# The last four weight chunks of a routed expert block: half of their pieces issued from ScalarE's DMA queue

## Chip, cores and metric

One NeuronCore of a Trainium2 chip runs the whole program. The metric is device time in microseconds (us); a version is timed in several runs, and the median counts. TensorE (PE) multiplies, VectorE (DVE) and ScalarE (ACT) do elementwise work, GpSimd (POOL) little, SyncE (SP) only issues DMA transfers. The profile's times count from the start of the span.

## What is computed

One encoder layer over 512 tokens of width 1024: token mixers, a layer norm, then a mixture of 32 SwiGLU experts, two for each token, and a second layer norm. The change touches the experts alone:

```python
def expert_block(args):
    tok, wgt, e = args
    xb = t[tok]
    hb = jax.nn.silu(xb @ w_gate[e]) * (xb @ w_up[e])
    return (hb @ w_down[e]) * wgt[:, None].astype(xb.dtype)
...
return _layer_norm(ALPHA * h + ffn, ln2_g[layer], ln2_b[layer])
```

All 32 experts are used, each with 6 MB of float32 weights (gate and up 1024 x 512, down 512 x 1024).

## The kernel before

**Rounds.** The experts are taken in 15 rounds (`PER`, L32): two or four experts a round share the 128 rows of the PE array. The last round, p = 14, has four experts with 32 token slots each. A round is: gather its tokens, gate projection, up projection (`gate_up`, L1175), silu and product (`glu`), transposes, the down projection in two halves of 512 output columns, and adding the results to the tokens' rows (`combine`).

**Chunks.** The weights come in chunks of 1 MB, 192 in all, numbered in the order of use; the last round has chunks 168 to 191: eight of gate (168 to 175), eight of up (176 to 183), four for the first down half (184 to 187) and four for the second (188 to 191). A gate or up chunk holds half of one expert's rows. PE takes the row blocks k = 0 to 3 of all four experts first (chunks 176 to 179 of up), then k = 4 to 7 (180 to 183). `chunk_load` (L713) issues a chunk: gate and up as one transfer of 1 MB (L726), chunks 184 to 187 as two halves of 512 KB (L738), and chunks 188 to 191 as four pieces of 256 KB each (L743): halves `kk` = 0, 1 and in each two pieces `j` = 0, 1, a piece being 256 rows x 256 columns of one expert. `PLACE[p] + 2 * kk + j` is the piece's place in the experts' order; which expert stands there is known only at run time, so `expert` (L703) loads its number from the tile `cnti` into a register of SP (a TENSOR_LOAD, L707).

**Buffers.** Chunks go round a ring of SBUF buffers (`ring_at`); from chunk 174 on, a chunk takes the buffer of the chunk 14 before it. Chunks 188 and 189 take those of gate chunks 174 and 175 (tiles sX and craw), 190 and 191 those of up chunks 176 and 177 (two tiles sS). A load waits until PE has read the older chunk. `load_after(n)` (L781) issues, in the program's order, all loads whose buffer is free once the chunks below n are used; `gate_up` calls it after gate (m = 0) and after up (m = 1), `pair` after the down halves.

**Queue and semaphores.** All these loads are issued by SP, in order. The DMA transfers of the program take eight semaphores (DMAHW0 to DMAHW7) in turn, and each transfer's issue waits until the transfer that had its semaphore before has landed; so eight are in flight at most, and an issue that waits holds back all issues behind it on its engine.

**The end.** `last_round` (L1502) prepares the rows of the second layer norm (four small casts on ACT, `row_parts`), then slot numbers, silu and product, three spread rows that ACT copies (L1520), transposes, the first down half (`down_mm`, chunks 184 to 187), its combination, and the second half in four column blocks (`columns`, L1540, chunks 188 to 191), one chunk each. `finish` does the layer norm and stores.

Of the kernel before, what the change touches and what calls it, by code (L numbers as in the profile page):

```python
# [24 lines left out]
E = 32  # L25
# [10 lines left out]
PLACE = [sum(PER[:p]) for p in range(len(PER))]  # L36
# [7 lines left out]
def dram(ap, offset, dims):  # L44
    return bass.AP(tensor=ap.tensor, offset=ap.offset + offset, ap=dims)
# [3 lines left out]
def hybrid_block(ctx: ExitStack, tc: tile.TileContext, x, w_in, b_in, sg_ln_g, sg_ln_b, sg_w, sg_b,  # L49
# [3 lines left out]
    nc = tc.nc  # L53
# [618 lines left out]
    def ring_at(i):  # L672
        if i < 22:
            return ring[i - 2]
        if i >= LAST:
            return ring_at(LAST - 14 + (i - LAST) % 14)
        return (ring[:13] + ["raw"] + ring[13:])[(i - 22) % AHEAD]
# [14 lines left out]
    NP = len(PER)  # L692
    order = [(p, c) for p in range(NP) for c in range(6 * PER[p])]
    where = {pc: i for i, pc in enumerate(order)}

    def wide(i):
        p, c = order[i]
        return p > 0 and (c < 4 * PER[p] or p < NP - 1)

    ids = {}  # L700


    def expert(place):  # L703
        if place < FIXED:
            return slice(place, place + 1)
        if place not in ids:
            ids[place] = nc.values_load(  # L707
                cnti[0:1, E + 1 + place:E + 2 + place], engines=[mybir.EngineType.SP], min_val=0, max_val=E - 1,
                skip_runtime_bounds_check_because="a sum of a one-hot column's products with 0 to 31")
        return ds(ids[place], 1)  # L710


    def chunk_load(dst, i, kk):  # L713
        p, c = order[i]
        n = PER[p]
        if wide(i):
            e, part = expert(PLACE[p] + c % n), c // n % 2
            src = w_down if c >= 4 * n else (w_gate, w_up)[c // (2 * n)]
            dst = dst.rearrange("p k a b -> p (k a b)" if kk is None else "p a b -> p (a b)")
            run = dst.shape[1]  # L720
            at = run * kk if kk else 0
            if c >= 4 * n:
                rows, at = slice(0, FF), at + 2048 * part
            else:
                rows = slice(512 * part, 512 * part + 512)
            nc.sync.dma_start(dst, src[0][e, rows, :].rearrange("o (p i) f -> p (o i f)", i=4)[:, at:at + run])  # L726
            return
        if p == 0 and c < 8:
            nc.sync.dma_start(dst, dram((w_gate, w_up)[c // 4], (2 * p * D + 256 * (c % 4) + 128 * kk) * FF,
                                        [[FF, 128], [D * FF, 2], [1, FF]]))  # L730
        elif p == 0:
            nc.sync.dma_start(dst, dram(w_down, (2 * p * FF + 256 * (c % 2) + 128 * kk) * D + 512 * ((c - 8) // 2),
                                        [[D, 128], [FF * D, 2], [1, 512]]))
        else:
            m, q = (c - 16) // 4, c % 4
            if m == 0:
                w, r = w_down[0][expert(PLACE[p] + 2 * (q % 2) + kk)], 256 * (q // 2)
                nc.sync.dma_start(dst, w[:, r:r + 256, 0:512].rearrange("o (k p) f -> p (o k) f", p=128))  # L738
            else:
                r, f = 256 * (q % 2), 512 + 256 * (q // 2)  # L740
                for j in range(2):
                    w = w_down[0][expert(PLACE[p] + 2 * kk + j)]
                    nc.sync.dma_start(dst[:, j].rearrange("p (k f) -> p k f", f=256),  # L743
                                      w[:, r:r + 256, f:f + 256].rearrange("o (k p) f -> p (o k) f", p=128))

    held, whole = {}, {}
# [34 lines left out]
    def load_after(n):  # L781
        if 24 <= n < len(order):
            i = max(chunks) + 1
            while i < len(order) and max(v for v in chunks if v > 1 and ring_at(v) == ring_at(i)) < n:
                load_chunks(i, i + 1)
                i += 1
# [72 lines left out]
    cnti = const.tile([1, 2 * E + 1], I32, name="cnti")  # L859
# [315 lines left out]
    def gate_up(p, xe, filler=None):  # L1175
        pg, pu = bank("acc"), bank("acc")
        n = PER[p]
        w = 128 // n
        for m, o in enumerate((pg, pu)):

            ks = range(8) if p or m else (3, 4, 5, 0, 1, 6, 2, 7)
            for k in ks:
                if filler and m and k % 2:
                    filler(k // 2)
                for j in range(n):
                    P.matmul(o[j * w:(j + 1) * w, :], lhsT=xe[:, k, j * w:(j + 1) * w],  # L1186
                             rhs=chunk(p, m, j, k), start=k == ks[0], stop=k == ks[-1],
                             skip_group_check=True)
            if p == 1:
                load_chunks(32 + 5 * m, 37 + 4 * m)  # L1190
            load_after(where[p, 2 * n * (m + 1) - 1] + 1)
        return pg, pu

    with tc.manual_schedule():
# [76 lines left out]
    def glu(pg, pu, scale=1.0 / WSCALE):  # L1271
        sl = mw.tile([128, FF], F32, name="sl", tag="olo")
        S.activation(sl, pg, AF.Silu)  # L1273
        V.scalar_tensor_tensor(sl, sl, scale, pu, op0=OP.mult, op1=OP.mult)  # L1274
        return sl
# [226 lines left out]
    def last_round(gu, ohf):  # L1502
        G.memset(ones_r.bitcast(F32), 1.0)
        G.memset(zero_b, 0.0)
        p = NP - 1
        l2 = ln2_params()

        spare = [spare_at(i) for i in range(1, 3)]
        for tag in spare:
            held.pop(tag, None)  # L1510
        v, more = [slot(tag, F32R) for tag in spare]
        ov = [(v[:, 0], v[:, 1]), (v[:, 2], v[:, 3])]
        parts = [row_parts(l2[j // 2][0:1, j % 2], *[w[0:1] for w in places])
                 for j, places in enumerate(ov + [(more[:, 0], more[:, 1]), (more[:, 2], more[:, 3])])]
        tid, ws = slot_info(p, ohf, "acc")
        sl = glu(*gu)
        for j in range(3):
            pb = bank("acc")
            spread(parts[j], pb)
            S.copy(l2[j // 2][:, j % 2], pb)  # L1520
        hT = glu_transpose(sl, "acc", wide=False)
        ohT = token_hot(tid)
        S.activation(warm2, eps_c, AF.Sqrt)

        def split_out(n, po, cs):
            oh, ol = [w[:, cs] for w in ov[n]]
            S.activation(oh, po[:, cs], AF.Copy, scale=ws)
            V.scalar_tensor_tensor(ol, po[:, cs], ws, oh.bitcast(F32), op0=OP.mult, op1=OP.subtract)

        def combine1(cs, stop=False):  # L1530
            for h in range(2):
                for t in range(NT):
                    P.matmul(pc[t][:, cs], lhsT=ohT[:, t * 128:(t + 1) * 128], rhs=ov[1][h][:, cs],
                             start=False, stop=stop and h == 1, skip_group_check=True)

        def columns(po, m):
            cs = slice(256 * (m // 2), 256 * (m // 2) + 256)
            for k in range(m % 2 * 2, m % 2 * 2 + 2):
                for j in range(4):
                    P.matmul(po[j * 32:(j + 1) * 32, cs], lhsT=hT[:, k, j * 32:(j + 1) * 32],  # L1540
                             rhs=chunks[where[p, 20 + m]][j // 2][:, j % 2, k % 2 * 256:k % 2 * 256 + 256],
                             start=k == 0, stop=k == 3, skip_group_check=True)

        most, rest = slice(0, 256), slice(256, 512)
        split_out(0, down_mm(p, 0, hT), slice(0, 512))
        for t in range(NT):
            p0 = bank("acc")
            for h in range(2):
                P.matmul(p0, lhsT=ohT[:, t * 128:(t + 1) * 128], rhs=ov[0][h], start=h == 0, stop=h == 1)
            V.tensor_add(y[t][:, 0:512], y[t][:, 0:512], p0)  # L1550
            V.bn_stats(st2[t][:, 0], y[t][:, 0:512])
        po = [bank("acc"), bank("acc")]
        pz = [bank("acc") for _ in range(2)]
        columns(po[0], 0)
        for t in range(2):
            spread(parts[3], pz[t], skip_group_check=True)
        columns(po[0], 1)
        split_out(1, po[0], most)
        columns(po[1], 2)
        combine1(most)  # L1560
        for t in range(NT):
            V.bn_stats(st2[t][:, 1], pc[t][:, most])
        pz += [bank("acc") for _ in range(2)]
        spread(parts[3], pz[2], skip_group_check=True)
        columns(po[1], 3)
        split_out(1, po[1], rest)
        combine1(rest, stop=True)
        spread(parts[3], pz[3], skip_group_check=True)
        return l2, pz
# [107 lines left out]
```

## Time and profile before

| | us |
|---|---|
| median of 3 runs (934.21 to 934.65) | 934.59 |
| the profiled execution | 934.43 |
| its span | 932.9 |
| PE busy in the span | 891.9 (96%) |
| DVE, ACT, POOL busy | 430.9, 292.8, 58.0 |
| mean DMA rate over the span | 275 GB/s |

The span holds the program's instructions; the 1.5 us between it and the execution's time lie around it. Busy shares are means over stages with different limits, so a change at the very end is read from the rows of the last 75 us. In the chain of waits, a row is a stretch of work or of waiting that the end hangs on; a DMA in it counts from its issue to its landing. Matmul rows show the engine's start of a group and, in brackets, how long it sat idle before and what ended that.

### The profile page before, as it was taken

How to read it: one execution, taken by the hardware profiler on the slowest of the kernel's cores; microseconds unless marked ns; L12 is line 12 of the kernel's file. 1: busy time of each engine (PE TensorE's matmuls, PEld its weight loads, DVE VectorE, ACT ScalarE, POOL GpSimd, SP SyncE). 2: the span in 40 equal slices, each digit the busy share in tenths (PEclk: the TensorE clock that was granted, in tenths of full speed). 3: DMA queues.
4: the chain of work that ended last, by engine and by line, in shares of the span. 5: the costliest groups of instructions: out<-in, count | busy, mean ns of one | idle time of the engine just before them, and what ended most of it. 6: DMA issues, size and time to landing. Idle time of an engine off the chain costs nothing. (4 is left out here: it accounts for less than half of the span.)

```text
span 932.9 us, 13620 instructions
## 1 busy us (share of the span) xinstructions
PE 891.9 (96%) x5215; PEld 577.4 (62%) x5216; DVE 430.9 (46%) x912; ACT 292.8 (31%) x526; POOL 58.0 (6%) x114
## 2 busy tenths in 40 slices
PE   8999999999999999999999999799999999978786
PEld 6989898986888888888834544344444444422132
DVE  4567675767963243244778422322333223401216
ACT  4456575667841242133361101110111011100112
POOL 6010101001010020020000000000000000000002
PEclk9999999999999999999999999899999999988899
DMA  8635343533233386874688999999999999999993
GB/s 227 169 100 145 97 136 96 136 113 102 69 98 95 89 319 217 290 259 160 260 293 340 402 417 410 416 419 419 418 420 419 420 420 418 418 418 420 420 359 142
DMA packets 79446, 256.11 MB, mean 275 GB/s; under 512 B 8984, under 2 KB 30544, under 8 KB 58384
## 3 DMA queue, kind: packets, MB, share of 16 engines
q1 hardware_dynamic: 78064, 252.36, 71.7%
q0 software_dynamic: 1312, 2.83, 1.5%
q8 instruction: 43, 0.70, 0.3%
q14 instruction: 27, 0.22, 0.1%
HBM read 244.67 MB, written 2.10 MB: 265 GB/s over the span
## 5 line engine op out<-in xcount | busy, mean ns | idle before, releaser
L119 DVE TENSOR_TENSOR sW<-wraw,sW 128x1024 fp32r<-128x1024 f32 (+1 forms) x38 | 46.5, 1224 | 98.4 <-ACT sW L118 98.3
L118 ACT CAST sW<-wraw 128x1024 fp32r<-128x1024 f32 (+1 forms) x38 | 39.1, 1030 | 116.9 <-PE ps_w L144 63.3
L1186 PE MATMUL ps_acc<-sS,xe 128*64 128x512 f32 (+1 forms) x192 | 65.9, 613 | 8.0 <-PEq L1317 5.8
L142 PE MATMUL ps_acc<-sX,sW 128*128 128x512 f32 x184 | 73.3, 398 | 0.0
L144 PE MATMUL ps_acc<-sX,sW 128*128 128x512 f32 x184 | 72.3, 393 | 0.0
L143 PE MATMUL ps_acc<-sX,sW 128*128 128x512 f32 x184 | 72.0, 391 | 0.0
L1260 DVE TENSOR_REDUCE tid<-ps_w 128x1 f32<-128x2 f32 x12 | 1.9, 158 | 139.4 <-PE ps_w L1255 139.4
L1303 DVE SCALAR_TENSOR_TENSOR olo<-ps_acc,ws,ohi 128x512 fp32r<-128x512 f32 x24 | 18.0, 750 | 99.3 <-ACT ohi L1302 99.3
L1313 DVE TENSOR_TENSOR h<-h,ps_w 128x512 f32<-128x512 f32 x96 | 59.4, 679 | 8.5 <-PE ps_w L1310 8.5
L1186 PE MATMUL ps_acc<-sW,xe 128*64 128x512 f32 (+1 forms) x152 | 60.6, 617 | 1.4 <-DMA sW<-in_w_up_dram 1.4
L1186 PE MATMUL ps_acc<-sO,xe 128*64 128x512 f32 (+1 forms) x224 | 59.6, 594 | 0.0
L1302 ACT ACTIVATE ohi<-ps_acc,ws 128x512 fp32r<-128x512 f32 x24 | 16.5, 687 | 130.5 <-PE ps_acc L1293 117.9
L1245 PEld LDWEIGHTS <-hs 128*128 128x128 f16 x768 | 44.5, 98 | 19.8 <-issue 19.6
L1186 PE MATMUL ps_acc<-sX,xe 128*64 128x512 f32 (+1 forms) x152 | 47.9, 645 | 4.3 <-DMA sX<-in_w_up_dram 3.4
L1245 PE MATMUL ps_acc<-oh,hs 128*128 128x128 f16 x768 | 51.1, 220 | 0.0
L1186 PE MATMUL ps_acc<-sE,xe 128*64 128x512 f32 (+1 forms) x176 | 48.9, 594 | 1.3 <-DMA sE<-in_w_up_dram 1.3
L262 DVE TENSOR_TENSOR sW<-wraw,sW 128x1024 fp32r<-128x1024 f32 x31 | 38.3, 1241 | 11.0 <-ACT sW L258 10.3
L1186 PEld LDWEIGHTS ps_acc<-sS,xe 128*64 128x64 f32 (+1 forms) x192 | 18.1, 129 | 38.2 <-issue 32.2
L1284 ACT COPY hT<-ps_w 128x512 f32<-128x512 f32 x12 | 7.0, 585 | 107.8 <-PE ps_w L1281 107.8
L1273 ACT ACTIVATE sl<-ps_acc 128x512 f32<-128x512 f32 x13 | 7.7, 595 | 104.0 <-PE ps_acc L1186 104.0
L1293 PE MATMUL ps_acc<-sS,hT 128*64 128x512 f32 (+1 forms) x96 | 37.3, 627 | 2.2 <-DMA sS<-in_w_down_dram 2.2
L144 PEld LDWEIGHTS ps_acc<-sX,sW 128*128 128x128 f32 x184 | 34.5, 188 | 7.5
(405 smaller groups left out, 2011.2 us busy)
## 6 DMA issues: line engine op xcount, KB each, us to landing
wraw<-in_w_in_dram SPq DMA_DIRECT2D x32, 512.0 KB, 3.7
sO<-in_w_up_dram SPq DMA_DIRECT2D x14, 1024.0 KB, 19.8
sS<-in_w_gate_dram SPq DMA_DIRECT2D x13, 1024.0 KB, 17.3
sX<-in_w_down_dram SPq DMA_DIRECT2D x13, 1024.0 KB, 14.6
sS<-in_w_down_dram SPq DMA_DIRECT2D x12, 1024.0 KB, 17.4
sE<-in_w_gate_dram SPq DMA_DIRECT2D x12, 1024.0 KB, 19.8
sS<-in_w_up_dram SPq DMA_DIRECT2D x11, 1024.0 KB, 17.3
sO<-in_w_gate_dram SPq DMA_DIRECT2D x11, 1024.0 KB, 19.8
```

Of the source, the lines that this page charges most:

```text
L118: S.copy(hi, src)
L119: V.tensor_sub(lo, src, hi.bitcast(F32))
L142: P.matmul(o, lhsT=lh, rhs=rh, start=first, stop=False)
L143: P.matmul(o, lhsT=lh, rhs=rl, start=False, stop=False)
L144: P.matmul(o, lhsT=ll, rhs=rh, start=False, stop=last)
L262: V.tensor_sub(usplit[i][1], uraw[i], usplit[i][0].bitcast(F32))
L1186: P.matmul(o[j * w:(j + 1) * w, :], lhsT=xe[:, k, j * w:(j + 1) * w], rhs=chunk(p, m, j, k), start=k == ks[0], stop=k == ks[-1], skip_grou ...
L1245: P.matmul(pg[d // 4][:, (d % 4) * 128:(d % 4 + 1) * 128], lhsT=part_block(hs[t][j], d), rhs=ohf[:, t], start=d % 4 == 0 and t == 0 and j ...
L1293: P.matmul(po[j * w:(j + 1) * w, :], lhsT=hT[:, k, j * w:(j + 1) * w], rhs=chunk(p, 2 + n, j, k), start=k == 0, stop=k == 3, skip_group_ch ...
L1302: S.activation(oh, po, AF.Copy, scale=ws)
L1303: V.scalar_tensor_tensor(ol, po, ws, oh.bitcast(F32), op0=OP.mult, op1=OP.subtract)
L1313: V.tensor_add(yn, yn, pcs[t])
```

## The change

In chunks 188 to 191 the pieces of the second half (`kk` = 1) are issued by ACT, on ACT's DMA queue; the expert numbers they need are loaded into registers of ACT as well. The first halves stay with SP. In the last round, the loads that become possible after up (chunks 190 and 191) are no longer written behind up in `gate_up`, but in `last_round` behind `glu`, so on ACT they stand after silu.

```diff
-    def expert(place):
+    def expert(place, engine=mybir.EngineType.SP):
         if place < FIXED:
             return slice(place, place + 1)
-        if place not in ids:
-            ids[place] = nc.values_load(
-                cnti[0:1, E + 1 + place:E + 2 + place], engines=[mybir.EngineType.SP], min_val=0, max_val=E - 1,
+        if (place, engine) not in ids:
+            ids[place, engine] = nc.values_load(
+                cnti[0:1, E + 1 + place:E + 2 + place], engines=[engine], min_val=0, max_val=E - 1,
                 skip_runtime_bounds_check_because="a sum of a one-hot column's products with 0 to 31")
-        return ds(ids[place], 1)
+        return ds(ids[place, engine], 1)
...
                 for j in range(2):
-                    w = w_down[0][expert(PLACE[p] + 2 * kk + j)]
-                    nc.sync.dma_start(dst[:, j].rearrange("p (k f) -> p k f", f=256),
+                    queue, engine = ((nc.sync, mybir.EngineType.SP), (nc.scalar, mybir.EngineType.Activation))[kk]
+                    w = w_down[0][expert(PLACE[p] + 2 * kk + j, engine)]
+                    queue.dma_start(dst[:, j].rearrange("p (k f) -> p k f", f=256),
                                       w[:, r:r + 256, f:f + 256].rearrange("o (k p) f -> p (o k) f", p=128))
...
             if p == 1:
                 load_chunks(32 + 5 * m, 37 + 4 * m)
-            load_after(where[p, 2 * n * (m + 1) - 1] + 1)
+            if p < NP - 1 or m == 0:
+                load_after(where[p, 2 * n * (m + 1) - 1] + 1)
...
         sl = glu(*gu)
+        load_after(where[p, 15] + 1)
         for j in range(3):
```

ACT's order in the last round, the change (sO3 and sZ0 take the casts, sl is silu's output; the rows that prepare a transfer's address are left out):

```order
L707 TENSOR_LOAD cnti_2781
...
L744 DMA sX3_3783<-in_w_down_dram 128x2x256 [waits DMAHW4_49,DMAHW0_49,PE_49]
...
L744 DMA sX3_3783<-in_w_down_dram 128x2x256 [waits DMAHW2_49,PE_49]
...
L744 DMA craw_4014<-in_w_down_dram 128x2x256 [waits DMAHW6_49,DMAHW7_49,DMAHW3_49,DMASW7_49]
...
L744 DMA craw_4014<-in_w_down_dram 128x2x256 [waits DMASW0_49,PE_49]
L118 CAST sO3_8027<-sO2_3509 1x512 [waits DMAHW7_49,DMASW1_49]
...
L1275 ACTIVATE sl_8053<-ps_acc_7929 128x512 [waits DVE_49]
...
L744 DMA sS0_4009<-in_w_down_dram 128x2x256 [waits DMAHW7_49,DMAHW1_49,PE_49]
...
L744 DMA sS0_4009<-in_w_down_dram 128x2x256 [waits DMAHW2_49,PE_49]
...
L744 DMA sS1_4011<-in_w_down_dram 128x2x256 [waits DMAHW4_49]
...
L744 DMA sS1_4011<-in_w_down_dram 128x2x256 [waits DMAHW5_49,PE_49]
L1523 COPY sO2_3509<-ps_acc_8064 128x512 [waits PE_49]
```

Before, none of the DMA rows stood there. The semaphores that the eight new transfers take themselves are, in turn, 0, 2, 3, 4 and, behind silu, 1, 2, 4, 5.

SP's order from the second up chunk to the second down chunk, before (sS1 to sE0 are up chunks 177 to 183, sE1 and sE2 down chunks 184 and 185):

```order
L726 DMA sS1_4011<-in_w_up_dram 128x2048 [waits DMAHW0_49,PE_49]
...
L726 DMA sW2_4018<-in_w_up_dram 128x2048 [waits DMAHW1_49,PE_49]
...
L726 DMA sS2_4193<-in_w_up_dram 128x2048 [waits DMAHW2_49,PE_49]
...
L726 DMA sW0_4195<-in_w_up_dram 128x2048 [waits DMAHW3_49,PE_49]
...
L726 DMA sS3_4197<-in_w_up_dram 128x2048 [waits DMAHW4_49,PE_49]
...
L726 DMA sW1_4199<-in_w_up_dram 128x2048 [waits DMAHW5_49,PE_49]
...
L726 DMA sE0_3265<-in_w_up_dram 128x2048 [waits DMAHW6_49,PE_49]
...
L738 DMA sE1_3268<-in_w_down_dram 128x2x512 [waits DMAHW7_49]
...
L738 DMA sE1_3268<-in_w_down_dram 128x2x512 [waits DMAHW0_49,PE_49]
...
L738 DMA sE2_3271<-in_w_down_dram 128x2x512 [waits DMAHW1_49]
```

and the same rows in the change:

```order
L726 DMA sS1_4011<-in_w_up_dram 128x2048 [waits DMAHW1_49,PE_49]
...
L726 DMA sW2_4018<-in_w_up_dram 128x2048 [waits DMAHW5_49,PE_49]
...
L726 DMA sS2_4193<-in_w_up_dram 128x2048 [waits DMAHW6_49,PE_49]
...
L726 DMA sW0_4195<-in_w_up_dram 128x2048 [waits DMAHW7_49,PE_49]
...
L726 DMA sS3_4197<-in_w_up_dram 128x2048 [waits DMAHW0_49,PE_49]
...
L726 DMA sW1_4199<-in_w_up_dram 128x2048 [waits DMAHW3_49,PE_49]
...
L726 DMA sE0_3265<-in_w_up_dram 128x2048 [waits DMAHW6_49,PE_49]
...
L738 DMA sE1_3268<-in_w_down_dram 128x2x512 [waits DMAHW7_49]
...
L738 DMA sE1_3268<-in_w_down_dram 128x2x512 [waits DMAHW0_49,PE_49]
...
L738 DMA sE2_3271<-in_w_down_dram 128x2x512 [waits DMAHW1_49]
```

SP's transfers keep their order, but their semaphores move: ACT's transfers take numbers between them. sW2 now waits for the semaphore of the first half of gate chunk 175, sS3 for that of ACT's first piece, sW1 for ACT's third, and sE2's two halves for ACT's fifth and sixth.

## Rows read from the trace of the kernel before

**Rows 1.** The page's slices: GB/s in 40 equal slices of the span

```profile
GB/s 227 169 100 145 97 136 96 136 113 102 69 98 95 89 319 217 290 259 160 260 293 340 402 417 410 416 419 419 418 420 419 420 420 418 418 418 420 420 359 142
```

**Rows 2.** The chain that ended last, 870 to 933: start us, us, what

```profile
872.75 19.82 DMA sE<-in_w_up_dram
...
892.62 1.05 PE ps_acc L1186 x2
...
897.63 1.00 PE ps_acc L1186 x8
...
901.85 3.69 PE ps_acc L1293 x32
...
915.40 1.04 PE ps_acc L1540 x16
```

**Rows 3.** PE's waits, 895 to 933: line, releaser, us in total, times, longest

```profile
PE ps_acc L1549 <- ACT sO L1527: 0.8, 1, 0.8
...
PE ps_acc L1453 <- DVE h L1550: 0.4, 1, 0.4
```

**Rows 4.** Single DMA issues at 875.12, 892.69, 893.94, 909.42: KB, us to landing

```profile
sE<-in_w_down_dram SPq DMA_DIRECT2D x1, 512.0 KB, 18.8
...
sO<-in_w_down_dram SPq DMA_DIRECT2D x1, 512.0 KB, 10.7
...
sX<-in_w_down_dram SPq DMA_DIRECT2D x1, 256.0 KB, 10.1
...
sS<-in_w_down_dram SPq DMA_DIRECT2D x1, 256.0 KB, 5.4
```

**Rows 5.** Timeline of SP's queue, 872 to 911: start us, us, instruction

```profile
875.12 0.39 SPq L738 DMA_DIRECT2D sE<-in_w_down_dram  x1
...
892.69 0.39 SPq L738 DMA_DIRECT2D sO<-in_w_down_dram  x1
893.94 0.41 SPq L743 DMA_DIRECT2D sX<-in_w_down_dram  x1
...
904.18 5.62 SPq L743 DMA_DIRECT2D sS<-in_w_down_dram  x8
...
909.42 0.37 SPq L743 DMA_DIRECT2D sS<-in_w_down_dram  x1
```

**Rows 6.** Timeline of PE, 845 to 905: start us, us, [idle before and releaser]

```profile
875.24 1.02 PE L1186 MATMUL ps_acc<-sS,xe 128*32 128x512 f32 x2 [0.22 <-DMA sS<-in_w_up_dram]
877.65 1.04 PE L1186 MATMUL ps_acc<-sS,xe 128*32 128x512 f32 x2 [1.38 <-DMA sS<-in_w_up_dram]
880.14 1.92 PE L1186 MATMUL ps_acc<-sW,xe 128*32 128x512 f32 x2 [1.45 <-DMA sW<-in_w_up_dram]
...
892.62 1.05 PE L1186 MATMUL ps_acc<-sE,xe 128*32 128x512 f32 x2 [1.30 <-DMA sE<-in_w_up_dram]
...
903.59 1.90 PE L1293 MATMUL ps_acc<-sO,hT 128*32 128x512 f32 x16
```

**Rows 7.** Line 707, 800 to 933: duration ns min/median/max, first and last start

```profile
L707 SPq TENSOR_LOAD <-cnti x4: 268/270/275, 834.2 to 839.5; - x4
```

**Rows 8.** Timeline of ACT, 840 to 933

```profile
875.06 0.60 ACT L1273 ACTIVATE sl<-ps_acc 128x512 f32<-128x512 f32 x1 [8.95 <-PE ps_acc L1186]
899.61 1.56 ACT L1520 COPY sO<-ps_acc 128x512 f32<-128x512 f32 x3 [23.95 <-PE ps_acc L1453]
```

**Rows 9.** DMA issues at 822.6 (POOL) and 821 to 822 (SP): KB, us to landing

```profile
sO<-in_ln_g_dram POOLq DMA_DIRECT2D x1, 4.0 KB, 4.9
...
sS<-in_w_down_dram SPq DMA_DIRECT2D x1, 1024.0 KB, 17.7
```

**Rows 10.** Windows: busy us of PE, PEld, DVE, ACT, POOL; PEclk, DMA share, GB/s

```profile
880.00:885.00 5.00, 4.28 (x5) 0.87 (x6) 0.00 (x0) 0.00 (x0) 0.00 (x0) 0.50 1.01 421
893.00:898.00 5.00, 5.00 (x26) 1.17 (x28) 0.00 (x0) 0.00 (x0) 0.00 (x0) 1.00 1.05 383
900.00:910.00 10.00, 8.20 (x64) 3.48 (x62) 3.86 (x7) 3.93 (x7) 0.00 (x0) 1.00 0.99 320
```

## The prediction

> **What bounds the kernel now.** I read the page's slices first: from about 513 to 886 us, the rate stands at 402 to 420 GB/s in every slice of 23.3 us [rows 1]. The expert weights arrive as fast as they are ever seen to arrive, and whatever the kernel needs at the end needs its place in that stream.
>
> Second, the chain of waits in order of time [rows 2]. Until 892.57 it is a DMA: the last up chunk of the last round (the eighth of eight), issued at 872.75, landed 19.8 us later. From there the chain is compute alone: 6.0 us of up projection, then silu's product, transposes, the first down product at 901.85, combining, statistics, the norm. Nothing in it waits for a DMA again, and PE's longest wait after 895 is 0.8 us, for ACT [rows 3].
>
> Third, how near the later chunks are. Landings come from single issues [rows 4, 5]. First half of the first down chunk: 875.12 + 18.8 = 893.9. Last half of the fourth: 892.69 + 10.7 = 903.4; PE reads it from 903.6 on, without a wait [rows 6]. So it came just in time, with 0.2 us to spare. The first piece of the last four chunks lands at 893.94 + 10.1 = 904.0, the last at 909.42 + 5.4 = 914.8, and PE reads it from 915.4 on [rows 2]. Two prices follow: seven half chunks of 512 KB in 903.4 - 893.9 = 9.5 us, 1.36 us each; fifteen 256 KB pieces in 10.8 us, **0.72 us** each.
>
> **The change, part by part.**
>
> Issues taken from SP: SP loses 8 issues. Its last eight take 5.62 us, 0.70 us each [rows 5], while pieces land every 0.72 us. SP issues some ahead of need (5.4 to 10.1 us before landing), so issuing costs the path nothing today, and taking it away gives nothing. A rule of the Trainium skill speaks against the change (DMA: Bandwidth & Descriptors, "Issuing engines are not separate DMA queues"): a second issuing engine saves only the sequencer's time to issue. By it the change can give at most 8 issues of SP's time, and no bandwidth.
>
> Work added on ACT: two register loads (0.27 us each on SP [rows 7]) and 8 issues (0.37 us each, 0.70 us apart [rows 5]): 6.1 us. ACT is idle 9.0 us before silu and 24.0 us after it [rows 8], so this costs nothing by itself. If the first four push the four small casts and silu back by about 6 us, silu ends near 881; its product needs the up half, done at 898.6. That cover would be gone only if ACT still stood at its last four issues when the copies at 899.6 come.
>
> When the pieces go out; this is the cost. SP is in order, so before the change the pieces queue behind all up and down chunks. On ACT's queue only ACT's own order and the buffers hold them. The first four (second halves of chunks 188 and 189) reuse the buffers of gate chunks 174 and 175, free when PE ends gate at about 875 (the first up matmul starts at 875.24 [rows 6]). At that time seven of the eight up chunks are still on their way. The second four (190 and 191) sit behind silu and reuse up chunks 176 and 177, whose second halves PE has read by about 890 (it runs out of data at 891.3, 1.30 us ahead of the last up chunk [rows 6]). At that time the four down chunks of the first output half have not landed.
>
> Whether they overtake: a POOL transfer of 4 KB issued at 822.6 landed in 4.9 us while a 1 MB chunk that SP issued in the microsecond before took 17.7 us [rows 9]: a second queue does not stand behind SP's backlog. So I take it that all eight pieces of ACT are served before the last half down chunk. A piece that shares the engines is bounded by 256 KB at the best rate of rows 1, 420 GB/s, 0.62 us, and by 256 KB at the 320 GB/s of 900 to 910 [rows 10], 0.82 us. I take 0.72, the spacing of landings, the nearest row.
>
> **The sum.** Last up chunk: 4 x 0.72 = 2.9 us later, 895.5. Last half down chunk: 8 x 0.72 = 5.8 us later, 909.2. PE reaches the first down product at 901.85 + 2.9 = 904.8, works through its first half (1.7 us, 901.85 to 903.59 in rows 2 and 6) and then waits for data from 906.5 to 909.2. Against 903.6 this is **+5.6 us** (4.8 to 6.4 by the two prices). What follows is the compute chain of rows 2, moved as a whole. SP's 8 remaining pieces land by 909.2 + 5.8 = 915.0, as today, and are wanted 5.6 us later than today: no wait there. Sum: 934.43 + 5.6 = 940.0 for an execution like the profiled one. The median shown, 934.59, lies 0.16 above it, so the forecast is **940.2**.
>
> Waits that the new order adds: the order shows that SP's and ACT's transfers now take the same eight semaphores in turn, each waiting for the transfer that had its semaphore before. The sixth up chunk (sS3) therefore waits until ACT's first piece has landed, the seventh (sW1) for ACT's third, and both halves of the second down chunk (sE2) for the fifth and sixth, which wait for PE. Instead of eight transfers SP then has three to five in flight. Up chunks land 2.5 us apart (PE starts on them at 877.65 and 880.14 [rows 6]), so that is 7 to 12 us of work. I cost this at nothing, because that much keeps the engines busy. What it costs if a piece lands late is the first rival.
>
> **The rivals.**
>
> **1.** The queue runs dry, or TensorE falls to its lower clock (0.28). If ACT's pieces get a small share beside SP's big chunks, the third lands only after SP's three remaining chunks. The engines then idle about one issue-to-first-byte time, which no row shows apart; a 4 KB transfer takes 4.9 us in all [rows 9], and half of it is my estimate, 2.4 us. Also, PE idles longer between up chunks. In 880 to 885 the granted clock was 0.50, the 1.2 GHz level, after PE had waited 1.4 us for each of two chunks [rows 6, 10]; if it falls again for the last part of up, those 6.0 us grow by up to 6. With the last up chunk at 895.5 + 2.4 and 3 us more of PE time, up ends at 898.6 + 2.9 + 2.4 + 3 = 906.9 and the end moves by 8.3 us: **942.9**. With one of the two, 941 to 942. For it: rows 10, and the semaphore order. Against: the last part of up runs at 1.00 today, in 893 to 898. The Trainium skill (same page, "Queues, rings and completion order") says that each engine goes round its queues packet by packet; with small packets on ACT's queue this would favour this rival. Nothing here shows two loaded queues side by side.
>
> **2.** Only the first four overtake (0.10). If the second four find the down chunks already under way, the last half down chunk moves by four pieces, 2.9 us, and the end by 2.7 to 2.9: **937.4**. Against: they are released some 13 us before that chunk's landing.
>
> **3.** Not slower: the pieces ride in gaps (0.08). If one queue leaves room on the engines that a second one fills, up chunks land when they do now and pieces cost nothing. The room needed is 1 MB between 875 and 892.6, some 60 GB/s on top of 420. If it is there, the chain of rows 2 stays: 934.6, or at best without the 0.4 us PE waits for DVE at 911 [rows 3], 934.2. It decides at 0.25 us per piece: there the end moves by 8 x 0.25 - 0.2 = 1.8 us, and below that no slowing can be told. Against: no slice of rows 1 exceeds 420 GB/s.
>
> **How the numbers follow.** Forecast 0.54, rivals 0.28, 0.10, 0.08. A measurement of this kernel can tell a change of about 0.2%, 1.9 us. The first three cases lie beyond that: slower 0.92. Rival 3 splits into same 0.06 and faster 0.02. The forecast's own range is 939.4 to 941.0 by the prices of a piece. To leave out 2 in 10 at most, the range takes in the second rival's 937.4 and the first up to 1.6 us past its sum, for a piece at 0.82 us instead of 0.72 and another stretch at the lower clock: 937.0 to 944.5.
>
> **What would show it.** Right: ACT has four issues at 875 to 878 and four at about 889 to 896; the last up chunk lands near 895.5 and the last of the four down chunks near 909; PE waits 2 to 3 us for a DMA inside the first down product, where now it waits for none; from there the rows of the end stand as before, some 5.6 us later. Wrong: up chunks that land when they do now (rival 3); a rate well below 380 GB/s between 880 and 900 or a granted clock of 0.50 after 895 (rival 1); the second four landing after the down chunks (rival 2).

## The result, and the profile after

The changed kernel takes 942.56 us (median of four runs, 940.73 to 942.74), the kernel before beside it 934.62: ratio 1.0078 [1.0064, 1.0092], slower by 7.9 us. The profiled execution is the one of 940.73, its span 939.2. Of the kernels in the experiments below, pool_queue and move_alone each had one execution of 4963 us where all others took 933 to 944; the ratios leave these two out. In the new listing L1186, L1293, L1453, L1520, L1540 and L743 are L1187, L1295, L1455, L1523, L1543 and L744.

The page's slices, GB/s, answer to [rows 1]:

```profile
GB/s 226 175 96 140 96 135 101 138 105 103 66 113 97 97 306 226 291 266 171 233 327 334 404 412 419 415 419 419 418 420 418 420 420 418 418 418 418 377 340 90
```

From the 23rd to the 37th slice (up to 868 us) the rate is 404 to 420, as it was before (402 to 420); the 38th (868 to 892) has 377, where the 38th before (863 to 886) had 420. No slice passes 420: the second queue added no rate.

The chain that ended last (start us, us, what) answers to [rows 2]:

```profile
874.72 12.19 DMA craw<-in_w_down_dram
...
887.60 7.86 DMA sE<-in_w_up_dram
...
895.50 1.04 PE ps_acc L1187 x2
...
900.51 1.00 PE ps_acc L1187 x8
...
902.44 7.44 DMA sO<-in_w_down_dram
...
909.92 1.92 PE ps_acc L1295 x10
...
921.70 1.04 PE ps_acc L1543 x16
```

Two DMAs are new in it. ACT's third piece (craw, landed 886.9) now stands ahead of the last up chunk, which is issued only at 887.60; before, it was issued at 872.75. And the last half down chunk, landing at 902.44 + 7.44 = 909.88, now sets when the first down product ends. PE's timeline shows how (start, us, instruction, idle before):

```profile
895.50 1.04 PE L1187 MATMUL ps_acc<-sE,xe 128*32 128x512 f32 x2 [1.84 <-DMA sE<-in_w_up_dram]
...
904.74 3.25 PE L1295 MATMUL ps_acc<-sE,hT 128*32 128x512 f32 x16 [0.68 <-ACT hT L1286]
907.81 1.79 PE L1295 MATMUL ps_acc<-sO,hT 128*32 128x512 f32 x6
909.92 1.90 PE L1295 MATMUL ps_acc<-sO,hT 128*32 128x512 f32 x10 [0.32 <-DMA sO<-in_w_down_dram]
```

ACT's timeline answers to [rows 8]:

```profile
872.99 1.43 ACTq L744 DMA_DIRECT2D sX<-in_w_down_dram  x2
874.72 1.20 ACTq L744 DMA_DIRECT2D craw<-in_w_down_dram  x2
876.01 1.14 ACT L118 CAST sO<-sO 1x512 fp32r<-1x512 f32 x2 [14.12 <-PE ps_acc L1187]
...
878.09 0.58 ACT L1275 ACTIVATE sl<-ps_acc 128x512 f32<-128x512 f32 x1
888.84 3.58 ACTq L744 DMA_DIRECT2D sS<-in_w_down_dram  x4
902.49 1.56 ACT L1523 COPY sO<-ps_acc 128x512 f32<-128x512 f32 x3 [23.82 <-DMA sE<-in_w_down_dram]
```

ACT has room: its last issue ends 10 us before its next copy. What waits is SP, in its timeline and its waits (line, releaser, us in total, times, longest):

```profile
874.80 0.33 SPq L726 DMA_DIRECT2D sW<-in_w_up_dram  x1
882.98 0.33 SPq L726 DMA_DIRECT2D sS<-in_w_up_dram  x1
887.02 0.33 SPq L726 DMA_DIRECT2D sW<-in_w_up_dram  x1
887.60 0.33 SPq L726 DMA_DIRECT2D sE<-in_w_up_dram  x1
```

```profile
SPq L726 <- DMA craw<-in_w_gate_dram: 10.0, 2, 9.2
SPq L738 <- DMA sS<-in_w_down_dram: 8.3, 3, 5.7
SPq L726 <- DMA sX<-in_w_down_dram: 7.6, 1, 7.6
SPq L726 <- DMA craw<-in_w_down_dram: 3.5, 1, 3.5
```

SP stood 7.6 us behind ACT's first piece and 3.5 us behind its third, the semaphore order of the change. It also stood 9.2 us behind the first half of gate chunk 175 before any piece had gone out, and 8.3 us, in three waits, behind ACT's last four pieces. What that did to the engines is in the windows, which answer to [rows 10]:

```profile
880.00:885.00 5.00, 3.89 (x5) 0.50 (x5) 0.00 (x0) 0.00 (x0) 0.00 (x0) 0.52 1.01 359
887.00:891.00 4.00, 4.00 (x28) 1.00 (x29) 0.00 (x0) 0.00 (x0) 0.00 (x0) 1.00 0.85 293
```

In 887 to 891 the DMA share is 0.85 at 293 GB/s, where it was 1.01 at 399 before: for some 0.6 us the engines had nothing to do. SP's long wait for ACT's fifth piece (to 896.6) shows no such hole: in steps of 2 us the share reads 0.98 to 1.07 from 889 to 903. In this trace a wait of SP cost time only where little else was in flight.

### The profile page after: what moved, and what is told of

The parts are those of the page before. It is cut to its first block, busy times and chain, and to the rows that moved or that the text cites. A ratio compares the mean times of both kernels' runs of the same rounds, so it can differ in the third digit from the quotient of the medians.

```text
span 939.2 us, 13626 instructions
## 1 busy us (share of the span) xinstructions
PE 894.0 (95%) x5215; PEld 577.3 (61%) x5216; DVE 431.3 (46%) x912; ACT 292.8 (31%) x526; POOL 58.0 (6%) x114
## 3 DMA queue, kind: packets, MB, share of 16 engines
q0 software_dynamic: 1312, 2.83, 1.5%
q10 hardware_dynamic: 2176, 2.10, 0.7%
## 5 line engine op out<-in xcount | busy, mean ns | idle before, releaser
L1187 PE MATMUL ps_acc<-sS,xe 128*64 128x512 f32 (+1 forms) x192 | 66.1, 614 | 8.4 <-PEq L1319 5.9
L1187 PE MATMUL ps_acc<-sW,xe 128*64 128x512 f32 (+1 forms) x152 | 61.8, 619 | 2.8 <-DMA sW<-in_w_up_dram 2.8
L1187 PE MATMUL ps_acc<-sO,xe 128*64 128x512 f32 (+1 forms) x224 | 60.1, 594 | 0.2 <-DMA sO<-in_w_gate_dram 0.2
L1187 PE MATMUL ps_acc<-sX,xe 128*64 128x512 f32 (+1 forms) x152 | 47.8, 649 | 5.3 <-DMA sX<-in_w_up_dram 3.8
L1187 PE MATMUL ps_acc<-sE,xe 128*64 128x512 f32 (+1 forms) x176 | 48.9, 594 | 1.8 <-DMA sE<-in_w_up_dram 1.8
L1187 PEld LDWEIGHTS ps_acc<-sS,xe 128*64 128x64 f32 (+1 forms) x192 | 18.1, 130 | 38.7 <-issue 32.4
L144 PEld LDWEIGHTS ps_acc<-sX,sW 128*128 128x128 f32 x184 | 34.5, 188 | 7.5
L143 PEld LDWEIGHTS ps_acc<-sX,sW 128*128 128x128 f32 x184 | 34.6, 188 | 6.1
L142 PEld LDWEIGHTS ps_acc<-sX,sW 128*128 128x128 f32 x184 | 34.6, 188 | 6.2
```

Of the source, the lines that this page charges most:

```text
L142: P.matmul(o, lhsT=lh, rhs=rh, start=first, stop=False)
L143: P.matmul(o, lhsT=lh, rhs=rl, start=False, stop=False)
L144: P.matmul(o, lhsT=ll, rhs=rh, start=False, stop=last)
```

## The experiments

Three groups of kernels ran on other chips, each with its own runs of the kernel before (medians 936.08, 936.12 and 935.2). Single runs of the kernel before spread there from 933.3 to 939.6, so an execution's own time says little about 2 us. Part of that spread lies before the change's place: the first up chunk of the last round lands anywhere from 874.4 to 879.1 us in the traces. So beside the ratios I measure from that landing, in each trace, to the landing of the last up chunk, to that of the last half down chunk, and to the end of the span. A landing is an issue's start plus its time to landing, as in the chain: 887.60 + 7.86 = 895.46, less 874.68, gives 20.78.

| kernel | ratio, 95% | first up chunk lands at | to last up | to last half down | to the end |
|---|---|---|---|---|---|
| before | | 875.11 | 17.46 | 28.24 | 57.76 |
| the change | 1.0078 [1.0064, 1.0092] | 874.68 | 20.78 | 35.20 | 64.48 |
| again | 1.0075 [1.0048, 1.0103] | 874.51 | 20.82 | 34.99 | 64.57 |
| move_alone | 1.000 [0.9986, 1.0015] | 876.20 | 17.50 | 28.24 | 57.77 |
| pool_queue | 1.0058 [1.0038, 1.0079] | | | | |
| pool_again | 1.0069 [1.0043, 1.0094] | 877.36 | 20.51 | 34.30 | 63.58 |
| thin_pieces | 1.0037 [1.0023, 1.0051] | 876.38 | 19.30 | 33.13 | 62.41 |
| thin_columns | 1.0037 [1.0021, 1.0052] | 876.60 | 19.21 | 34.34 | 63.60 |
| pool_thin | 1.0017 [0.9998, 1.0036] | 874.62 | 18.95 | 30.95 | 60.50 |
| first_four | 1.0051 [1.0035, 1.0068] | 876.06 | 20.45 | 33.76 | 63.01 |
| second_four | 1.0045 [1.0027, 1.0063] | 878.05 | 17.78 | 31.67 | 60.94 |
| late_four | 1.0024 [1.0003, 1.0046] | 879.07 | 17.47 | 28.18 | 61.41 |
| pool_late | 1.0009 [0.9991, 1.0026] | 874.39 | 17.43 | 28.24 | 59.26 |

**Two theories.** Bytes: the pieces go out ahead of chunks that PE wants earlier, and each takes its time from them. Link: SP's issues wait for ACT's transfers in the turn of semaphores, and the queue runs dry.

**again**: the changed kernel once more, on another chip.

> The changed kernel once more. Its four times were 940.73 and three of 942.46 to 942.74, and the trace shown is the one of 940.73. By the theory of the stream order the data comes the same in both kinds (last half down chunk about 6.3 us later than before), and the 1.8 us between them are PE time at the lower clock after the data is there: a trace near 942.6 has the lower clock over the second half of the first down product and the combining behind it. The rival (the queue runs dry by a different amount) would show the last half down chunk itself landing 1.8 us later. Time 940.5 to 942.8.

The slowing is there, 1.0075, and the three distances agree with the first trace within 0.21 us. The hole is there too: a DMA share of 0.59 in 887 to 889. The four runs took 940.65 to 943.83, and the profiled one is that of 940.65, so what the expectation says of a trace near 942.6 is not settled.

**move_alone**: the kernel before, with only the place of the load call changed.

```diff
-            load_after(where[p, 2 * n * (m + 1) - 1] + 1)
+            if p < NP - 1 or m == 0:
+                load_after(where[p, 2 * n * (m + 1) - 1] + 1)
...
+        load_after(where[p, 15] + 1)
```

> The kernel before with one part of the change: the loads of the last two chunks are written behind silu instead of behind up, all on SP. SP's order is the same, so both theories say 934.6, within 0.5.

Ratio 1.000, all distances within 0.04 us. Where the call stands is worth nothing; what counts is the queue.

**pool_queue** and **pool_again**: the same pieces at the same place in the program, on POOL's queue, whose transfers take other semaphores (DMASW), so that SP's turn has none of them in it.

```diff
-                    queue, engine = ((nc.sync, mybir.EngineType.SP), (nc.scalar, mybir.EngineType.Activation))[kk]
+                    queue, engine = ((nc.sync, mybir.EngineType.SP), (nc.gpsimd, mybir.EngineType.Pool))[kk]
```

> The same eight pieces on POOL's queue. POOL's transfers take semaphores of their own, so SP's transfers keep the turn of the kernel before and wait for no piece; only the place of the pieces in the stream of data remains. Theory of the stream order (eight pieces of 0.72 us ahead of the last half down chunk): 940 to 942, the last up chunk some 2.9 us and the last half down chunk some 5.8 us later than before. Theory of the semaphores (SP held back by ACT's pieces): 934.6, up to 1 more.

> The eight pieces on POOL's queue once more, for its trace. Both theories alone have shown a part so far: bytes ahead in the stream without the semaphores' link cost about 4.5 us, the link with an eighth of the bytes 3.4 us. Stream order: SP issues as in the kernel before, eight transfers in flight, and the last half down chunk still lands some 5 us later than before, with the engines never idle (419 GB/s or near it from 875 to 895).

pool_queue left no trace of an ordinary execution (its six others took 938.59 to 943.57); pool_again is the same kernel. Its SP timeline and chain:

```profile
872.44 0.33 SPq L726 DMA_DIRECT2D sS<-in_w_up_dram  x1
873.71 0.33 SPq L726 DMA_DIRECT2D sW<-in_w_up_dram  x1
874.99 0.33 SPq L726 DMA_DIRECT2D sE<-in_w_up_dram  x1
877.37 12.98 SPq L738 DMA_DIRECT2D sE<-in_w_down_dram  x4
```

```profile
874.99 22.88 DMA sE<-in_w_up_dram
...
898.00 13.65 DMA sO<-in_w_down_dram
...
911.70 1.92 PE ps_acc L1295 x10
```

The last up chunk is issued early again, as in [rows 2], and yet takes 22.88 us where it took 19.82. Windows of the same trace:

```profile
880.00:885.00 5.00, 2.60 (x4) 0.20 (x3) 0.00 (x0) 0.00 (x0) 1.79 (x5) 0.80 1.02 396
885.00:890.00 5.00, 2.97 (x4) 0.68 (x4) 0.00 (x0) 0.00 (x0) 0.26 (x1) 0.50 1.02 403
```

No idle engine, no wait of SP for a piece, and still +3.05 us at the last up chunk and +6.06 at the last half down chunk. Four pieces, then eight: 0.76 us each both times. So most of the delay is there without the link. It is a matter of order: the last of all pieces lands 39.88 us after the first up chunk, where it landed at 39.70 before, so the stream as a whole lost only 0.2 us. In the change it lands at 40.99; 1.3 us are lost there. How much of the 0.76 us is bytes is not shown: 256 KB at 420 GB/s are 0.62 us, and the rate here is 396 and 403. POOL's transfers differ in one thing more: the eight pieces came in 640 packets (1952 of POOL's queue less the 1312 of before), on ACT's queue in 2176.

**thin_pieces** and **thin_columns** keep the link and cut ACT's bytes to an eighth, by rows or by columns. thin_columns ran after pool_thin below, whose 2.7 us its expectation uses.

```diff
-                    queue.dma_start(dst[:, j].rearrange("p (k f) -> p k f", f=256),
-                                      w[:, r:r + 256, f:f + 256].rearrange("o (k p) f -> p (o k) f", p=128))
+                    rows = slice(0, 16 if kk else 128)
+                    queue.dma_start(dst[rows, j].rearrange("p (k f) -> p k f", f=256),
+                                      w[:, r:r + 256, f:f + 256].rearrange("o (k p) f -> p (o k) f", p=128)[rows])
```

```diff
-                    queue.dma_start(dst[:, j].rearrange("p (k f) -> p k f", f=256),
-                                      w[:, r:r + 256, f:f + 256].rearrange("o (k p) f -> p (o k) f", p=128))
+                    n_ = 32 if kk else 256
+                    queue.dma_start(dst[:, j].rearrange("p (k f) -> p k f", f=256)[:, :, 0:n_],
+                                      w[:, r:r + 256, f:f + n_].rearrange("o (k p) f -> p (o k) f", p=128))
```

> ACT's eight transfers stay where they are, with the same semaphores and waits, but each carries 16 of its 128 partitions, an eighth of the bytes; the rest of these pieces is left out of the computation. Stream order: 8 x 0.09 = 0.7 us, so 935.3 (934.8 to 936). Semaphores: SP still waits for ACT's first and third piece before the sixth and seventh up chunk and for the fifth and sixth before the second down chunk, so most of the loss stays: 938 to 941.

> The change with an eighth of the bytes in ACT's eight pieces again, but as 32 of 256 columns in all 128 partitions (the rest of the pieces is left out of the computation), so that all engines carry alike. On POOL's queue, 16 of 128 partitions cost 2.7 us instead of the 0.7 of their bytes. If that came from an uneven load, the last half down chunk here lands at 28.2 + 0.7 + 2.2 (the link) = 31.1 us after the first up chunk; if it is the price of so many transfers of a second queue, at 33 or later as with 16 partitions on ACT.

With an eighth of the bytes the last half down chunk is still 4.9 and 6.1 us late. Windows of thin_columns:

```profile
880.00:885.00 5.00, 2.67 (x4) 0.35 (x4) 0.86 (x2) 0.39 (x1) 0.00 (x0) 0.68 0.90 326
885.00:890.00 5.00, 5.00 (x20) 0.95 (x18) 0.00 (x0) 0.00 (x0) 0.00 (x0) 0.63 0.82 271
...
900.00:905.00 5.00, 4.40 (x28) 1.82 (x27) 1.78 (x7) 2.12 (x4) 0.00 (x0) 1.00 0.88 275
```

The time of thin_pieces is at the low end of what its expectation gives for the link, 3.4 us above its own runs of before, and the landing in thin_columns is in the second of its two cases. Here the engines do run dry, to shares of 0.82 and 0.88. So the link has a price of its own, and I had put it at nothing. The 4.9 and 6.1 are not all its own: pool_thin has the eighth without the link and is 2.7 us late, which leaves 2.2 to the link in thin_pieces, and thin_columns still moves 2176 packets, as many as the change, where thin_pieces moves 384. The two prices do not add up: 2.2 by the link with few bytes, 0.9 with all of them (7.0 against pool_again's 6.1). That SP's standing still costs less while pieces keep the engines busy fits the windows of the change from 889 to 903; no run tests it alone.

**pool_thin**: thin_pieces on POOL's queue, neither the bytes nor the link.

> POOL's queue (own semaphores) and an eighth of the bytes (16 of 128 partitions of the eight pieces; the rest is left out of the computation): neither of the two costs. If these two are all there is, this is within 1 us of the kernel before. If a second queue costs by itself, 2 us or more above it.

Ratio 1.0017; the last half down chunk is 2.7 us late, where an eighth of eight pieces at 0.76 us would be 0.8. So eight thin transfers cost more than their bytes. The median lies between the two forecasts, and the trace is with the second. Nor were the engines idle: in 875 to 880 and 880 to 885 they are counted busy at 1.04 and 1.00, at 372 and 369 GB/s. Whether that comes from the few rows or from the transfers as such is not settled, since thin_columns kept the link and changed the packets.

**first_four** and **second_four**: only chunks 188 and 189, or only 190 and 191, give half their pieces to ACT.

```diff
-                    queue, engine = ((nc.sync, mybir.EngineType.SP), (nc.scalar, mybir.EngineType.Activation))[kk]
+                    queue, engine = ((nc.sync, mybir.EngineType.SP), (nc.scalar, mybir.EngineType.Activation))[kk if q < 2 else 0]
```

(second_four has `q > 1`.)

> Only the pieces of chunks 188 and 189 on ACT, those of 190 and 191 back on SP. Counted from the landing of the first up chunk of the last round (17.5 us to the last up chunk and 28.2 to the last half down chunk in the kernel before, 20.8 and 35.0 in the change): stream order says 20.4 and 31.1, the end 2.9 us late. The link adds what the engines idle while SP waits for ACT's first and third piece, 0.4 us in the change: 20.8 and 31.5. If the second four alone made the loss (3.4 us with them alone), 17.5 and 28.2.

> Only the pieces of the last two chunks (190, 191) on ACT, those of 188 and 189 back on SP. Stream order: up chunks land as before, four pieces (2.9 us) go ahead of the last half down chunk, the end moves by 2.7 us. Link: both halves of the second down chunk and two halves of the third and fourth wait for ACT's pieces, which wait for PE at about 890; SP then has the first down chunk alone in flight, the engines run dry for 1 to 3 us more, so 4 to 6 us in all, about as much as the whole change.

The first four alone push the last up chunk by 3.0 us, as forecast for them, but the last half down chunk by 5.5, not 3. Between the two landings the engines are counted busy at a lower rate (first_four, windows):

```profile
898.00:900.00 2.00, 2.00 (x18) 0.42 (x16) 0.00 (x0) 0.00 (x0) 0.00 (x0) 1.00 0.97 306
900.00:902.00 2.00, 2.00 (x18) 0.45 (x10) 0.00 (x0) 0.00 (x0) 0.00 (x0) 1.00 1.01 329
```

Before, the same kind of half chunks came at 373 to 386 GB/s (892 to 900). Why they came slower here is open. The second four alone leave the up chunks nearly where they were (+0.3) and cost the down chunks 3.4. There the link shows again: SP waits up to 6.0 us for a piece, and the share falls to 0.80 and 0.87 in the two steps of 897 to 901. Both groups do overtake; the parts, 5.5 and 3.4, are more than the whole, 7.0.

**late_four** and **pool_late**: the second four pieces are given out behind the transposes of the last round, when the last half down chunk is nearly in, by ACT or by POOL; the first four stay with SP.

```diff
         sl = glu(*gu)
-        load_after(where[p, 15] + 1)
...
+        load_after(where[p, 15] + 1)
```

(late_four also has the edit of second_four. pool_late also has a copy of one column of hT on POOL ahead of the call, so that POOL stands there until the transposes are done, and takes the pool_queue edit with `[kk if q > 1 else 0]`.)

> The same four pieces on ACT, but issued behind the load of the square-root table, at about 903, when the four down chunks are all on their way. Nothing goes ahead of a down chunk any more: the last half down chunk lands as before. SP's piece transfers take turns with ACT's, and the fourth of chunk 188 and three others wait for ACT's; they have some 1 to 2 us to spare. Both theories: within 1 us of the kernel before, up to 2 us above it if the pieces come too late for the last two column blocks.

> The pieces of chunks 190 and 191 on POOL's queue, held back by a one-column copy on POOL that needs the transposed product (about 902): own semaphores and nothing overtaken. Both costs are taken away: 17.5 and 28.2 us from the first up chunk to the last up and the last half down chunk, and the end as in the kernel before, within 0.5 us. If it is slower, the last two chunks come too late for their column blocks.

Both land their up and down chunks where the kernel before does, within 0.07 us: a piece that does not go out early costs those chunks nothing, link or not. late_four still loses at the end. ACT's first issue there is at 906.21, SP's fourth piece of chunk 188 waits for its turn with it, and the last piece lands 42.4 us after the first up chunk instead of 39.7. pool_late, without the link, is 1.0009 [0.9991, 1.0026] of the kernel before. The 1.5 us that its profiled execution has on top stand beside a stretch at the 1.2 GHz level in the first down product:

```profile
900.00:903.40 3.40, 2.73 (x16) 0.92 (x18) 0.05 (x1) 2.49 (x4) 0.79 (x2) 0.50 1.02 333
```

Its chain shows that product as 4.67 us of PE where [rows 2] have 3.69, which is 1.0 of the 1.5. No version ran faster than the kernel before.

## Why the prediction was right, and where it was short

Forecast was 940.2 us, slower by 5.6; measured were 942.56 by the median, slower by 7.9, and 940.73 in the profiled execution, slower by 6.3 than the 934.43 of before. The direction and the place of the loss came as forecast; the size came short by 0.7 us in the trace and by 2.4 in the median.

**When the pieces go out: right.** Forecast 875 to 878 and 889 to 896; ACT issued at 873 to 876 and 888.8 to 892.4. They overtook what SP had queued: all four first pieces landed by 890.1, before the sixth up chunk did.

**The price of a piece: right, slightly small.** Taken at 0.72 us from the spacing of landings; pool_again gives 0.76, inside the 0.62 to 0.82 of the two bounds, though with another form of packets than on ACT's queue.

**Last up chunk: right.** Forecast 895.5, landed 895.46. Part of that is luck: the stream began 0.43 us earlier in this execution, so the delay is 3.3, not 2.9.

**Last half down chunk: a little short.** Forecast 909.2, landed 909.88; from the first up chunk 7.0 us later, not 5.8. With the 0.24 us less that follows, the profiled execution adds up: -0.43 (first up chunk) + 3.32 (last up) + 3.64 (from there to the last half down) - 0.24 = 6.3.

**The step that failed** is "Waits that the new order adds: I cost this at nothing". I had named the right issues (sS3 behind the first piece, sW1 behind the third), but reasoned that 7 to 12 us of work in flight would keep the engines busy. The first piece took from 872.99 to 882.9, 10 us. SP had one or two transfers in flight from 883 to 887, not three to five (the fourth up chunk landed at 883.0 and the fifth at 885.9, and SP issued the sixth at 883.0 and the seventh at 887.0), and in 887 to 891 the share fell to 0.85. Against pool_again, which has the bytes and not the link, the change loses 0.3 us more at the last up chunk and 0.9 at the last half down chunk. That is the price of the link here as far as two traces give it, beside the 0.6 us of idle engines; POOL's other packets are part of the difference. The medians of pool_again and again (1.0069 and 1.0075) don't tell it from zero.

**Rival 1** thus came true in part, in its share and in its dry queue, though not in its price of 2.4 us. That the median, 942.56, lies beside its 942.9 is not shown to be its doing: the trace that we have is of 940.73, and its last part of up ran at a granted clock of 1.00 (893 to 898). Its share shows in the packets by queue, 875 to 883 and then 892 to 902 (queue, packets, MB, share of the engines' time; q1 is SP's, q10 is ACT's, with 2.10 MB in all on the page):

```profile
q1 hardware_dynamic: 371, 2.66, 81.0%
q10 hardware_dynamic: 569, 0.56, 20.2%
```

```profile
q1 hardware_dynamic: 1123, 2.72, 71.2%
q10 hardware_dynamic: 1088, 1.05, 31.5%
```

ACT had 17% of the bytes beside 1 MB chunks and 28% beside the last up chunks and half chunks. The Trainium skill (DMA: Bandwidth & Descriptors, "Queues, rings and completion order") says that an engine goes round its queues a packet at a time. If each packet of the profile is one turn, the second window agrees, 1123 packets to 1088, and the first does not: there ACT had more packets than SP, 569 to 371, and a sixth of the bytes. Rival 1's other half, a lower clock that costs, did not come in this trace, though its sign, 0.50 after 895, did: the granted clock was again at the 1.2 GHz level in 880 to 885, as before, and for 3.4 us in the first down product, where PE had to wait for the last half anyway:

```profile
904.00:907.40 3.40, 2.72 (x17) 0.69 (x18) 0.00 (x0) 2.13 (x4) 0.00 (x0) 0.51 1.05 368
```

That is also why PE's wait for a DMA reads 0.32 us and not the 2 to 3 forecast. The product took 904.74 to 911.8 instead of 3.69 us; slow matmuls filled most of the wait, and the chain names the DMA all the same.

**Rival 2** (only the first four overtake) falls: second_four alone costs 3.4 us. **Rival 3** (gaps that pieces fill) falls: no slice passed 420 GB/s. The Trainium skill's rule that a second issuing engine saves only issue time (same page, "Issuing engines are not separate DMA queues") held against any gain: no version ran faster.

**Open.** The other three runs of the changed kernel, 942.46 to 942.74, are 1.8 us above the profiled one, and no trace shows one of them; the runs of again spread as widely. Nor is it known why the parts sum to more than the whole, or why thin transfers cost more than their bytes.

## What to carry to other kernels

A second DMA queue gave this saturated stream no bytes; it changed their order. So price each transfer given to it as a delay to whatever is wanted next, and give out early only what is wanted early. Where the queues' transfers share a turn of semaphores, look up which issue on the old queue now waits for which transfer on the new one: a queue that never waited may run dry. When single executions scatter, measure in the trace from an event just ahead of the change.

## What the runs showed of the hardware that I had not expected

A 256 KB piece on a second queue beside 1 MB chunks took 10 us to land (872.99 to 882.9), about as long as three or four of SP's chunks took to pass (874.7, 877.2, 880.1 and 883.0). Most of the scatter between executions can lie ahead of the place that was changed: 4.5 us between pool_thin's and late_four's first up chunks (874.62 and 879.07), on one chip and in programs that are the same up to the last round. And engines that are counted busy do not always deliver alike: at shares of 0.97 to 1.01 half chunks came at 306 to 329 GB/s in first_four, where they had come at 373 to 386 before (892 to 900).
